# The delta rule's recurrence on one core: products of 64 partitions laid over all 128

## The chip, the cores and the metric

The kernel runs on one core of a Trainium2 chip. The metric is the time on the device in microseconds (us) for one execution, as the median of several runs. Nothing else runs on the chip.

## The reference

The model is two blocks on 512 tokens of 1024 features, in float32: a block with two attention branches and a layer of product-key experts, then a gated delta net and a short convolution. The change lies in the gated delta net alone, in its recurrence. It has 16 value heads that share 8 key heads in pairs, head width 128, and goes over the tokens in 8 chunks of 64:

```python
    def step(s, xs):
        q_c, k_c, u_c, w_c, qk_c, sd_c = xs
        v_new = u_c - jnp.einsum('bhck,bhkv->bhcv', w_c, s)
        o_c = jnp.einsum('bhck,bhkv->bhcv', q_c, s) + jnp.einsum('bhij,bhjv->bhiv', qk_c, v_new)
        s = s * sd_c[..., None, None] + jnp.einsum('bhck,bhcv->bhkv', k_c, v_new)
        return s, o_c
...
    _, o = lax.scan(step, s0, xs)
```

The state `s` of a head is 128 x 128 and is handed from chunk to chunk, so the chunks of a head are serial. `u_c` and `w_c` are the solutions of a 64 x 64 triangular system for each chunk and head.

## The kernel before, in words

One program runs four stages one after the other: `mix`, `peer`, `gdn`, `sconv`. All work of this study is in `gdn`, after its projections of keys and queries and after the inverse of the triangular systems. Tokens lie on partitions in tiles of 128, so one tile holds two chunks: chunk n has the partitions `o`, the lower 64 if n is even (`a_` = 0) and the upper 64 if it is odd (`a_` = 1). `RQ0` and `RQ1` hold for 8 heads each the inverse R (`RQ[:, 0]`) and the masked query-key product Q (`RQ[:, 1]`), as [128 partitions, 32 pairs of head and token tile, 64 columns]: the two chunks of a tile share a column block and lie on the two halves of the partitions.

`recur(kh, ...)` is a generator that takes the two value heads of key head kh through 8 chunks. It yields after each step that waits for another engine, 23 times in all; such a step is called a hop here. For every chunk but the first and last there are three:

- the state's product (L1510): keys and queries of the chunk, [128, 128] as the weights, times the state `Sx` of both heads in one product of 256 columns; then the output of the chunk before (L1495, Q times `vn`). VectorE answers with `rr` (L1513).
- L1518: R times `rr`, from the 64 partitions `o` onto the 64 partitions `o`. ScalarE answers with `vn` (L1519), then with two products for the output (L1522).
- L1529: `kd` times `vn`, from the 64 partitions `o` onto 128. VectorE answers with the new state `sn` (L1536, or L1533 for the first chunk).

The first chunk has no state: its L1518 reads `vb`. All products of the recurrence are float32, and TensorE runs each as two records of a load of weights and a matmul, so that the two heads of a hop make four.

TensorE's instructions stand in the order in which the code emits them (`manual_schedule`). A written plan places the hops: two key heads run at a time, one 12 steps of the plan behind the other, each has one hop in a step, and `fill` puts products of other projections in between: those of values and of the output gate (L207 to L209 on `x3h`, `x3l`: three float32r products of 512 columns for each row tile, 128 x 128 weights), and later of the output (the same lines on `ygh`, `ygl`, 256 columns). `prologue` starts a key head (transposes L1471 and L1480; `va`, the values, come by a DMA that GpSimd issues, L1477; VectorE makes `kd` and `vb`). `epilogue` and `epilogue2` end one (transposes L1558, then `ygh` on ScalarE, L1566). The other engines' order is set by the scheduler of the tile framework. Weights of the projections are loaded by SyncE and split in two parts by ScalarE (`whi`, L89) and VectorE or GpSimd (`wlo`, L92).

Of the kernel before, what the change touches and what calls it, by code (L numbers as in the profile page):

```python
# [29 lines left out]
def kernel(ctx: ExitStack, tc: tile.TileContext, A: dict, out: bass.AP):  # L30
# [24 lines left out]
    # ---------------------------------------------------------------- helpers  # L55
# [21 lines left out]
    share = {"every": 0, "n": 0}    # of the weights' second parts, every n-th by the pool engine  # L77

    def wchunk(ap, name="w"):
        """A [128, 2048] chunk of a weight matrix (8 row tiles, 256 columns) in two halves, each split  # L80
        into two float32r parts. For a token-major product the halves are along the rows, for a
        feature-major one along the columns."""
# [15 lines left out]
    def rsqrt(ss, n, shape, name="rs", dst=None):  # L98
        """1/sqrt(ss*n + eps): a first guess from the exponent's bits, then Newton steps."""
# [16 lines left out]
    def rsqrt2(ss, n, name, dst=None):  # L116
        """the same for two columns on the pool engine, by its power"""
        m = small.tile([P, 2], F32, name=name, tag=name)
        GP.tensor_scalar(m, ss, n, EPS, op0=ALU.mult, op1=ALU.add)
        r = m if dst is None else dst  # L120
        GP.tensor_tensor(r, m, mhalf, op=ALU.pow)
        return r
# [6 lines left out]
    def evac_split(hi, lo, p, scale):  # L129
        """hi + lo = p * scale, in two float32r parts."""  # L130
        S.activation(hi, p, AF.Copy, scale=scale)
        V.scalar_tensor_tensor(lo, p, scale, f32(hi), op0=ALU.mult, op1=ALU.subtract)
# [3 lines left out]
    class Stream:  # L136
        """The residual stream between two stages, [128, 4, 1024] token-major: in SBUF, in DRAM, 1/rms
        of every token, and the normed stream transposed, in two parts [128, 8, 512]. n: the stage
        that reads it."""
# [12 lines left out]
        def squares(self, tiles):  # L152
            """the sums of squares of every token of two token tiles"""
# [6 lines left out]
        def ready(self, t, ss):  # L160
            """token tiles t and t + 1 are complete; ss: their sums of squares"""
# [6 lines left out]
        def norm(self, t):  # L168
            """token tile t, normed and transposed"""
# [20 lines left out]
        def first_feat(self, ap, order=(0, 1)):  # L190
            """The token tiles of the second half, and proj_feat of the first chunk by halves."""
            w = [(m, *kview(x, NK)) for m, *x in wchunk(ap)]
            pp = [pj() for m in range(2)]
            for j in order:
# [4 lines left out]
                # The first start clears the whole bank.  # L199
# [28 lines left out]
    def proj_tok_last(aps, xs):  # L228
        """proj_tok whose token tiles end one after the other; yields them by pairs."""
# [22 lines left out]
    def proj_feat_steps(ap, xh, xl, by, n=T):  # L252
        """feature-major: [128 features, n tokens] for the two column tiles of a chunk."""
# [9 lines left out]
    def proj_tok_steps(aps, xs, by):  # L263
        """token-major: four [128 tokens, 256 columns]; aps: the chunks along K, xs: their operands."""
# [4 lines left out]
        # Two groups share a bank: the first matmul's start clears the whole bank, and the second  # L269
        # group's first write finds it cleared.  # L270
# [12 lines left out]
    # ---------------------------------------------------------------- token mixing  # L283
    def mix(X, O):
        w1 = A["w_in"]
        with ExitStack() as st:
# [56 lines left out]
            # ---- gated linear attention, head by head  # L343
# [5 lines left out]
            def gla_inside(h):  # L349
                """the parts of a head that need no state"""  # L350
# [94 lines left out]
            # ---- sliding window attention  # L445
# [31 lines left out]
            # Keys and queries in two float32r parts, feature-major: the keys' first part twice, on either  # L477
            # half of the partitions, and a query's two parts on the two halves; so one pass gives two of
            # the three products, and a second one the third. The second key head pair has the halves
            # swapped, for its keys' second part lies on the other half.  # L480
# [63 lines left out]
            def weights(n, hg, qT):  # L544
                """the softmax of four heads that share keys; the columns hold the tokens of block n up to the
                row and those of block n - 1 after it"""
# [57 lines left out]
            # ---- branch gates, output gate of the linear attention  # L604
# [31 lines left out]
            # Four heads a slot: their scores in one slot, the weighted sums two slots later; the tensor  # L636
            # engine's work in a fixed order, with the gates' projections in between.
# [31 lines left out]
            # ---- branches, merge  # L669
# [39 lines left out]
    # ---------------------------------------------------------------- product-key experts  # L709
    def peer(X, O):  # L710
        KD = 3                      # token tiles that go through all experts on the tensor engine
        ND = KD * P
        HS = 16                     # tokens of a staged block of gate matrices
        TB = 4                      # tokens of a block of one-hot rows
        with ExitStack() as st:
# [19 lines left out]
            # ---- the last token tile: its experts' rows by indirect DMA  # L735
# [37 lines left out]
            # ---- the other tiles through all experts: groups of five chunks, ten rows of experts  # L773
# [57 lines left out]
            # ---- scores and the 16 best keys of every head and half  # L831
# [36 lines left out]
            def route(t):  # L868
                """the 16 best experts of every head, their gates; yields every few operations"""
# [3 lines left out]
                # pairs (a, b) with (a+1)(b+1) <= 16: every other pair has 16 better or earlier ones  # L873
# [35 lines left out]
                # gates  # L909
# [21 lines left out]
                # indices and the gate's two parts, one row per (head, k), as float16  # L931
# [7 lines left out]
            def gate_matrices(t):  # L939
                """G[j, i] of every token of the tile, expert i * 128 + j"""  # L940
# [26 lines left out]
            # the tensor engine's projections at an even rate in between  # L967
# [41 lines left out]
    # ---------------------------------------------------------------- gated delta rule  # L1009
    def out_proj(aps, parts, X, O, wr, Y=None):  # L1010
        """X + rmsnorm(the projection (+ Y)) * w; aps[c]: the weights of 256 columns."""
# [38 lines left out]
    def conv_silu(p, wc, taps, tmp):  # L1050
        """Causal depthwise convolution along the free axis, one weight per partition and tap."""
# [7 lines left out]
    def gdn(X, O):  # L1059
# [6 lines left out]
        with ExitStack() as st:  # L1066
# [23 lines left out]
            # ---- keys and queries, feature-major and not normed: [dk, head, chunk, (k | q), 64]  # L1090
# [6 lines left out]
            def kq_mm(i):  # L1097
                """one tile of 128 columns of the projection; i: pair of key heads, (k, q), key head"""
# [26 lines left out]
            # ---- beta and g, token-major [128, 4, 16]  # L1125
# [53 lines left out]
            def g_rows():  # L1179
                # E[j, (h, t), i] = exp(G_i - G_j) for j <= i, else 0  # L1180
# [37 lines left out]
            def u_store(c, q):  # L1218
                """the diagonal blocks of U of key heads 2c and 2c + 1"""
# [8 lines left out]
            def rows(c):  # L1228
                """the factors of every token of key heads 2c and 2c + 1"""
# [56 lines left out]
            # ---- values (filler of the triangular solve)  # L1286
# [94 lines left out]
            # ---- R = (I + U)^-1: 32 x 32 diagonal blocks by substitution, (half, head, tile) on  # L1381
            # partitions
# [18 lines left out]
            # to rows on partitions by the tensor engine; the first block's transpose too  # L1401
# [12 lines left out]
            # the off-diagonal blocks: -R1 U12 R2; the two halves' blocks on a diagonal  # L1414
# [70 lines left out]
            def recur(kh, vb, kd, oo):  # L1485
# [15 lines left out]
                for n in range(8):  # L1501
# [26 lines left out]
                    for v in range(2):  # L1528
                        PE.matmul(B2[:, 1, v], kd[o, v, t, :], vn[o, v], start=True, stop=True)  # L1529
# [282 lines left out]
```

## Time and profile before

| what | value |
|---|---|
| median of 3 runs | 3065.36 us (3063.47 to 3077.59) |
| span of the profiled execution | 3072.8 us |
| TensorE busy over the span | 2943.9 us (96%) |
| VectorE, ScalarE, GpSimd busy | 1972.4, 1216.1, 662.6 us |
| recurrence, first to last product | 2246.8 to 2549.0 us of the span |
| TensorE, VectorE, ScalarE busy from 2246 to 2549 us | 294.9, 163.9, 123.2 us of 303.0 |
| mean granted TensorE clock there | 0.95 of full speed |

The profile gives for each instruction its engine, its start and its duration, and for each wait the engine that ended it. A matmul's end is modelled, so what a matmul costs is read from the start of one to the start of the next, or from the chain of work that ended last, in which the pieces follow one another without overlap. No time beyond its span is given for the profiled execution. It is 7.4 us longer than the median and lies within the runs shown.

### The profile page before, as it was taken

How to read it: one execution, taken by the hardware profiler on the slowest of the kernel's cores; microseconds unless marked ns; L12 is line 12 of the kernel's file. 1: busy time of each engine (PE TensorE's matmuls, PEld its weight loads, DVE VectorE, ACT ScalarE, POOL GpSimd, SP SyncE). 2: the span in 40 equal slices, each digit the busy share in tenths (PEclk: the TensorE clock that was granted, in tenths of full speed). 3: DMA queues.
4: the chain of work that ended last, by engine and by line, in shares of the span. 5: the costliest groups of instructions: out<-in, count | busy, mean ns of one | idle time of the engine just before them, and what ended most of it. 6: DMA issues, size and time to landing. Idle time of an engine off the chain costs nothing.

```text
span 3072.8 us, 42867 instructions
## 1 busy us (share of the span) xinstructions
PE 2943.9 (96%) x16274; PEld 2499.6 (81%) x16274; DVE 1972.4 (64%) x3798; ACT 1216.1 (40%) x2089; POOL 662.6 (22%) x583
## 2 busy tenths in 40 slices
PE   8999999998889999999899999999999999999998
PEld 6978778888889998777798888787866678888888
DVE  3348664499898776777787777658845554444432
ACT  3534473323345553333333333465343344332322
POOL 1001110002342312223454443134411202000000
PEclk9999999999999999999999999999999899999999
DMA  3213224333466779899999888446322313223222
GB/s 130 76 58 131 85 86 157 106 100 100 143 217 226 244 267 307 315 333 317 323 315 313 308 320 309 160 115 144 128 86 90 107 59 119 98 96 124 96 90 83
DMA packets 206919, 528.61 MB, mean 172 GB/s; under 512 B 38777, under 2 KB 84441, under 8 KB 202362
## 3 DMA queue, kind: packets, MB, share of 16 engines
q1 hardware_dynamic: 144018, 326.17, 32.5%
q0 software_dynamic: 43168, 155.27, 14.2%
q10 hardware_dynamic: 19528, 44.44, 3.9%
q8 instruction: 128, 2.10, 0.3%
q14 instruction: 77, 0.63, 0.1%
HBM read 464.49 MB, written 61.33 MB: 171 GB/s over the span
## 4 chain that ended last, share of the span: by engine, by line
PE 50%; DMA 9%; DVE 6%; issue 4%; ACT 2%; POOL 1%; SPq 0%; POOLq 0%; DVEq 0%; ACTq 0%
PE pp L207 12%; PE pp L208 11%; PE pp L209 11%; DMA wraw<-in_peer_v_dram 4%; DMA gath<-in_peer_v_rows_dram,ge 2%; PE ps L209 2%; PE ps L208 2%; PE ps L207 2%; DVE wlo L92 1%; PE ps L1495 1%; PE ps L1529 1%; DMA gath<-in_peer_u_rows_dram,ge 1%; DMA wraw<-in_peer_u_dram 1%; PE ps L954 1%; POOL gath L751 1%
## 5 line engine op out<-in xcount | busy, mean ns | idle before, releaser
L89 ACT ACTIVATE whi<-wraw 128x1024 fp32r<-128x1024 f32 x492 | 519.9, 1057 | 980.1 <-PE pp L208 555.1
L92 DVE TENSOR_TENSOR wlo<-wraw,whi 128x1024 fp32r<-128x1024 f32 x466 | 580.3, 1245 | 422.6 <-ACT whi L89 409.7
L209 PE MATMUL pp<-x2h,wlo 128*128 128x384 f32 (+2 forms) x1168 | 405.4, 347 | 23.7 <-DVE wlo L92 22.0
L207 PE MATMUL pp<-x2h,whi 128*128 128x384 f32 (+2 forms) x1168 | 407.6, 349 | 17.3 <-ACT whi L89 9.7
L208 PE MATMUL pp<-x2l,whi 128*128 128x384 f32 (+2 forms) x1168 | 404.2, 346 | 1.1 <-DVE x2l L188 1.1
L209 PE MATMUL ps<-whi,wtl 128*128 128x512 f32 x640 | 254.8, 398 | 8.5 <-DVE wtl L817 8.5
L208 PE MATMUL ps<-wlo,wth 128*128 128x512 f32 x640 | 254.9, 398 | 3.2 <-DVE wlo L92 3.2
L207 PE MATMUL ps<-whi,wth 128*128 128x512 f32 x640 | 253.8, 397 | 2.3 <-ACT whi L89 2.0
L209 PEld LDWEIGHTS pp<-x2h,wlo 128*128 128x128 f32 x1168 | 224.8, 193 | 34.7 <-DVE wlo L92 28.1
L751 POOL DMA_INDIRECT gath<-in_peer_u_rows_dram,ge x128 | 173.3, 1354 | 336.2 <-DVE gath L754 168.6
L207 PEld LDWEIGHTS pp<-x2h,whi 128*128 128x128 f32 x1168 | 225.3, 193 | 24.2 <-ACT whi L89 10.8
L751 POOL DMA_INDIRECT gath<-in_peer_v_rows_dram,ge x128 | 170.1, 1329 | 316.9 <-DVE gath L754 153.7
L208 PEld LDWEIGHTS pp<-x2l,whi 128*128 128x128 f32 x1168 | 225.2, 193 | 6.5 <-DVE x2l L188 1.6
L207 PE MATMUL pp<-x4h,whi 128*128 128x512 f32 (+1 forms) x528 | 202.4, 384 | 3.8 <-ACT x4h L187 3.8
L208 PE MATMUL pp<-x4l,whi 128*128 128x512 f32 (+1 forms) x528 | 202.7, 384 | 0.9 <-DVE x4l L188 0.9
L209 PE MATMUL pp<-x4h,wlo 128*128 128x512 f32 (+1 forms) x528 | 202.5, 384 | 0.0
L759 DVE SCALAR_TENSOR_TENSOR acc<-gath,w,acc 128x1024 f32<-128x1024 f32 x127 | 163.7, 1289 | 22.7 <-DMA gath<-in_peer_v_rows_dram,ge 22.5
L754 DVE SCALAR_TENSOR_TENSOR gath<-gath,grow 128x1024 f32<-128x1024 f32 x128 | 157.4, 1237 | 30.0 <-DMA gath<-in_peer_u_rows_dram,ge 29.8
L207 PE MATMUL pp<-x3h,whi 128*128 128x512 f32 (+1 forms) x400 | 168.4, 421 | 7.4 <-ACT x3h L187 5.7
L816 ACT ACTIVATE wth<-wt 128x384 fp32r<-128x384 f32 x128 | 66.8, 522 | 252.1 <-PE pp L208 154.5
L208 PE MATMUL pp<-x3l,whi 128*128 128x512 f32 (+1 forms) x400 | 156.4, 391 | 1.8 <-DVE x3l L188 1.8
L209 PE MATMUL pp<-x3h,wlo 128*128 128x512 f32 (+1 forms) x400 | 156.3, 391 | 0.0
(492 smaller groups left out, 6500.2 us busy)
## 6 DMA issues: line engine op xcount, KB each, us to landing
wraw<-in_peer_u_dram SPq DMA_DIRECT2D x128, 512.0 KB, 5.3
wraw<-in_peer_v_dram SPq DMA_DIRECT2D x128, 512.0 KB, 7.1
wraw<-in_sc_w_in_dram SPq DMA_DIRECT2D x64, 512.0 KB, 3.5
wraw<-in_w_in_dram SPq DMA_DIRECT2D x52, 512.0 KB, 4.0
Gd<-sgs ACTq DMA_DIRECT2D x24, 1024.0 KB, 6.5
wraw<-in_gdn_w_in_dram SPq DMA_DIRECT2D x48, 512.0 KB, 3.7
Gt<-Gd SPq DMA_DIRECT2D x12, 1920.0 KB, 15.8
Hd<-ht ACTq DMA_DIRECT2D x25, 384.0 KB, 4.5
```

Source lines behind the costliest of these rows:

```text
L89: S.activation(hi, raw, AF.Copy)
L92: (GP if pool_ else V).tensor_tensor(lo, raw, f32(hi), op=ALU.subtract)
L207: PE.matmul(p, lh, rh, start=first, stop=False, skip_group_check=skip)
L208: PE.matmul(p, lh, rl, start=False, stop=False, skip_group_check=skip)
L209: PE.matmul(p, ll, rh, start=False, stop=last, skip_group_check=skip)
L751: GP.indirect_dma_start(out=r, out_offset=None, in_=src, in_offset=bass.IndirectOffsetOnAxis(ap=idx3[:, k:k + 1], axis=0))
L754: V.scalar_tensor_tensor(r, r, 1.0, xn3, op0=ALU.mult, op1=ALU.mult, accum_out=h3[:, k:k + 1])
L759: V.scalar_tensor_tensor(acc3, r, w3[:, k:k + 1], acc3, op0=ALU.mult, op1=ALU.add)
L816: S.activation(wh, w, AF.Copy)
L954: PE.matmul(o, AB[:, 1, :, q], A2[:, 0, :, q], start=True, stop=False)
L1495: PE.matmul(B2[o, 0, v], Q[s_][o, u, :], vn[o, v], start=True, stop=True)
L1529: PE.matmul(B2[:, 1, v], kd[o, v, t, :], vn[o, v], start=True, stop=True)
```

## The change

Every product of the recurrence is made a product of 128 partitions onto 128. Two tiles for each of the two lanes (a lane is kh odd or even) and each parity of the chunk take the place of `rr` and `vn`: `rz` and `vz`. Their other half is set to zero once, by GpSimd, before the recurrence; each chunk writes its own half alone. `wide_mm` then takes 128 columns of `RQ` as weights: the chunk's own block of 64 and the block beside it, on the side that puts the wanted result on the chunk's own half of the output. The other half of the output receives a product that nobody reads. The first or last block of `RQ0` and `RQ1` has no such neighbour: there the product stays one of 64 output partitions (L1502). `kd` is taken on all 128 partitions, with the zeros of `vz` against the other chunk. The state's product of 256 columns becomes two of 128, one for each head. The first chunk's right side is now copied from `vb` into `rz` by VectorE (L1527). Comments and empty lines changed in many other places; they are left out here.

```diff
+            lanes = []
+            for i in range(2):
+                lanes.append([[tp.tile([P, 2, P], F32, name=n, tag="%s%d%d" % (n, i, a_)) for a_ in range(2)]
+                              for n in ("rz", "vz")])
+                for x in lanes[i]:
+                    for a_ in range(2):
+                        GP.memset(x[a_][64 * (1 - a_):64 * (1 - a_) + 64], 0.0)
+            RQ = [x.rearrange("p x u c -> p (x u c)") for x in (RQ0, RQ1)]
+
+            def wide_mm(out_, s_, u, a_, rhs):
+                c = 64 * (u - a_)
+                if 0 <= c <= 62 * 64:
+                    PE.matmul(out_, RQ[s_][:, c:c + P], rhs, start=True, stop=True)
+                else:
+                    PE.matmul(out_[64 * a_:64 * a_ + 64], RQ[s_][:, 64 * u:64 * u + 64], rhs, start=True, stop=True)
...
+                rz, vz = lanes[kh % 2]
...
-                        PE.matmul(B2[o, 0, v], Q[s_][o, u, :], vn[o, v], start=True, stop=True)
+                        wide_mm(B2[:, 0, v], s_, 32 + u, n % 2, vn[:, v])
...
-                    vn = r1("vn", 4)
+                    vn, r = vz[a_], rz[a_]
                     if Sx is None:
-                        r = vb[:, :, t, :]
+                        V.tensor_copy(r[o], vb[o, :, t, :])
                     else:
-                        r = r1("rr", 2)
-                        PE.matmul(B1[:, 0].rearrange("p v c -> p (v c)"), k_[:, n].rearrange("p x c -> p (x c)"),
-                                  Sx.rearrange("p v c -> p (v c)"), start=True, stop=True)
+                        for v in range(2):
+                            PE.matmul(B1[:, 0, v], k_[:, n].rearrange("p x c -> p (x c)"), Sx[:, v], start=True,
+                                      stop=True)
...
-                        PE.matmul(B1[o, 1, v], R[s_][o, u, :], r[o, v], start=True, stop=True)
+                        wide_mm(B1[:, 1, v], s_, u, a_, r[:, v])
...
-                        PE.matmul(B2[:, 1, v], kd[o, v, t, :], vn[o, v], start=True, stop=True)
+                        PE.matmul(B2[:, 1, v], kd[:, v, t, :], vn[:, v], start=True, stop=True)
```

On TensorE, at the start of the recurrence, the first hops of key head 0 stand so before the change (out<-in, output partitions x columns; `vn` and `rr` are the right sides, `RQ`, `kd` and `kq` the weights):

```order
L209 MATMUL pp<-x3h,wlo 128x512
L1518 MATMUL ps<-vb,RQ_17371 64x128 x2
L207 MATMUL pp<-x3h,whi 128x512
L208 MATMUL pp<-x3l,whi 128x512
L209 MATMUL pp<-x3h,wlo 128x512
L1529 MATMUL ps<-vn,kd 128x128 x2
...
L1510 MATMUL ps<-sn,kq_17370 128x256
L1495 MATMUL ps<-vn,RQ_17371 64x128 x2
```

and so after it:

```order
L209 MATMUL pp<-x3h,wlo 128x512
L1500 MATMUL ps<-rz,RQ_17371 128x128 x2
L207 MATMUL pp<-x3h,whi 128x512
L208 MATMUL pp<-x3l,whi 128x512
L209 MATMUL pp<-x3h,wlo 128x512
L1549 MATMUL ps<-vz,kd 128x128 x2
...
L1530 MATMUL ps<-sn,kq_17370 128x128 x2
L1500 MATMUL ps<-vz,RQ_17371 128x128 x2
```

Nothing moved on TensorE: each hop keeps its place between the same products of the projections, and only the shapes are others.

On GpSimd, between the inverse and the recurrence, the zeros stand ahead of the first loads of values:

```order
 L1419 MEMSET Tc 64x64x32 x2
 L92 TENSOR_TENSOR wlo<-wraw,whi 128x1024
-L1477 DMA va<-vd 128x512 x2
-L1560 DMA zl<-zd 128x512 x3
+L1494 MEMSET rz 64x256 x2
+L1494 MEMSET vz 64x256 x2
+L1494 MEMSET rz 64x256 x2
+L1494 MEMSET vz 64x256 x2
+L1477 DMA va<-vd 128x512 x2
+L1580 DMA zl<-zd 128x512 x3
```

The two loads `va`, which the first L1480 waits for, now stand behind eight more instructions.

On TensorE, where the two lanes meet without a projection between them and one chunk is the last block of its tile set, the rows after the change are these (`RQ_17371` is `RQ0`, `RQ_17392` is `RQ1`):

```order
L209 MATMUL pp<-x3h,wlo 128x512
L1530 MATMUL ps<-sn,kq_17370 128x128 x2
L1500 MATMUL ps<-vz,RQ_17371 128x128
L1502 MATMUL ps<-vz,RQ_17371 64x128
L1530 MATMUL ps<-sn,kq_17391 128x128 x2
```

One of four such products that keep their 64 output partitions stands here (L1502).

## Rows read from the trace of the kernel before

**Rows 1.** The page's head: busy us by engine (share of the span), instructions.

```profile
span 3072.8 us, 42867 instructions
PE 2943.9 (96%) x16274; PEld 2499.6 (81%) x16274; DVE 1972.4 (64%) x3798; ACT 1216.1 (40%) x2089; POOL 662.6 (22%) x583
```

**Rows 2.** Windows: length, busy (xcount) of PE, PEld, DVE, ACT, POOL; granted clock; DMA.

```profile
2246.00:2549.00 303.00, 294.91 (x1668) 207.49 (x1666) 163.93 (x445) 123.16 (x360) 43.41 (x53) 0.95 0.26 84
2344.00:2354.30 10.30, 9.78 (x30) 6.27 (x31) 2.98 (x8) 2.30 (x7) 1.14 (x3) 0.50 0.51 170
2419.00:2439.60 20.60, 20.59 (x63) 13.68 (x63) 5.57 (x18) 2.55 (x9) 2.67 (x5) 0.50 0.33 103
```

**Rows 3.** The chain that ended last: start us, us, what (records).

```profile
2302.89 1.02 PE ps L1480 x8
2303.92 0.23 PE pp L207
...
2304.62 0.64 PE ps L1529 x4
2305.26 0.43 PE pp L207
...
2306.15 0.57 PE ps L1510 x2
2306.72 0.58 PE ps L1495 x4
2307.29 0.43 PE pp L207
...
2308.19 0.87 PE ps L1558 x8
2309.06 0.58 PE ps L1518 x4
2309.64 0.43 PE pp L207
```

**Rows 4.** Waits, 2245 to 2550 us: who <- releaser: us, times, longest.

```profile
PEld pp L207 <- issue: 17.7, 96, 0.3
PEld ps L1529 <- ACT vn L1519: 7.2, 9, 1.6
PE ps L1529 <- ACT vn L1519: 4.1, 5, 1.4
```

**Rows 5.** The same chain where hops of both lanes meet.

```profile
2367.24 0.43 PE ps L1510 x2
2367.68 0.25 PE ps L1495
2367.93 0.01 PE ps L1518
2367.94 0.09 PE ps L1495
```

**Rows 6.** The chain at the start of key head 3.

```profile
2339.99 0.12 PE ps L1558
...
2344.09 0.39 ACT vn L1519
...
2344.52 1.22 PE ps L1529 x4
```

**Rows 7.** Ahead of the recurrence: timeline, a group by line, the tile va.

```profile
2237.88 1.16 POOL L1477 DMA_DIRECT2D va<-vd  x2
...
2242.79 1.30 PE L1480 MATMUL ps<-ident,va 128*128 128x128 f32 x8
...
L1421 POOL MEMSET Z<- 64x256 f32 x8 | 2.3, 308 | 0.1
...
DMA to landing us min/median/max: 4.0/4.4/4.8
```

**Rows 8.** Groups by line, VectorE, 2246 to 2549 us.

```profile
L1533 DVE COPY sn<-ps 128x128 f32<-128x128 f32 x16 | 4.0, 284 | 3.3 <-PE ps L1529 3.3
```

## The prediction

> **What bounds the kernel now.** I read the page's head first: TensorE is busy 96% of the span, no other engine over 64% [rows 1]. Then the windows of the recurrence: of 303.0 us TensorE is busy 294.9, VectorE 163.9, ScalarE 123.2 [rows 2]. So the stage ends when TensorE has issued its list, and the recurrence's serial answers are mostly covered by the projections between the hops. Busy is no proof of useful work, though, so I read the chain that ended last, whose pieces don't overlap [rows 3]. There the reader should compare two kinds of neighbours of the same projection. After a hop whose products use 64 rows or 64 columns of the array, L207 takes 0.43 us; after transposes that use all 128 x 128 (L1480 x8) it takes 0.23, which is its streaming. And four records of L1518 take 0.58, four of L1495 0.58, four of L1529 0.64, where eight float32 records of 128 columns with 128 x 128 weights (L1558 x8) take 0.87, 0.109 each. The dear thing is not the small product but going into and out of its shape. The waits agree: TensorE's weight loads stand idle before L207 96 times, 17.7 us in all, for "issue", which is nothing that the profile shows; of the waits that name another engine the longest are 7.2 us of weight loads and 4.1 of matmuls, both L1529 for ScalarE's `vn` [rows 4].
>
> **The change part by part.** *Shape switches removed.* One visit to a small hop costs 0.58 + 0.43 = 1.01 us with the L207 behind it [rows 3]. In full shape it is four records of 0.109, 0.44, and L207 at 0.23: 0.67. That saves 0.34. For L1529 it is 0.64 + 0.43 - 0.67 = 0.40. For the state's hop, L1510 x2 takes 0.43 where it needn't wait [rows 5], so 0.43 + 0.58 + 0.43 = 1.44 becomes eight records, 0.87, and 0.23: again 0.34. The two products of 128 columns cost what one of 256 did, 0.44 for 0.43. In TensorE's order of the program I count 156 runs of small hops between full-shape rows (184 hops, some next to each other), 42 of them entered by L1529. That gives 156 x 0.34 + 42 x 0.06 = 55.6 us. Seven of the runs end in the transposes L1471, whose 64 output columns stay another shape; their way out, 0.20, isn't saved: -1.4. Gross 54.2.
>
> *Side by side lost.* In six places an L1495 of one lane and an L1518 of the other follow each other on opposite halves. There the records alternate at 0.01 and 0.09 [rows 5]: eight take 0.56, and in full shape they take 0.87 one after the other. With L207 that is 0.99 now and 1.10 then: a loss of 0.11 where I booked a gain of 0.34, so I take off 6 x 0.45 = 2.7 us. [...] At its most, with all 512 records of R and Q two at a time, the loss would be 512 / 2 x 0.109 = 28 us instead of 2.7. But the four records of one visit don't overlap in the chain (0.58 for four), since both heads use the same half, so the sum goes by the row. [...]
>
> *Four products that keep 64 columns* (L1502): in and out of the shape again, 4 x 0.34 = 1.4 us lost.
>
> *Zeros ahead of the values.* Eight fills of 64 x 256 go in front of the first two loads `va` in GpSimd's queue. A fill of this shape takes 0.308 us [rows 7], together 2.5. `va` lands 4.0 to 4.8 us after its issue at 2237.9, so by 2242.7 at the latest, and L1480 starts at 2242.8: up to 0.9 us of slack. TensorE's order is fixed, so it stands still for 1.6 to 2.5 us; I take 2.0. GpSimd idled long before, but the fills stand behind its share of the weights in the queue. Nothing behind `va` is urgent (`zl` is for the epilogue).
>
> *Eight copies into `rz`.* 64 x 256 has no row; the nearest is a copy of 128 x 128 out of PSUM, 0.284 us [rows 8]. A first L1500 now waits for it, but it has three steps of the plan between `vb` and that product; the bounds are 0 and 8 x 0.28 = 2.3. I take 1.0, since VectorE may have other work before it.
>
> *Where the stall goes.* TensorE takes 303 us for about 116 steps of the plan, 2.6 us a step, and comes to a lane's next hop one step later. An answer is one or two operations of some 0.3 us plus what the engine has before them. With two visits cheaper in each step the next hop is due 0.4 to 0.7 us earlier, which a slack near 1 us mostly covers. Where it doesn't, the saving is lost: at the start of key head 3 the chain leaves TensorE at 2340.1, runs through VectorE and ScalarE (`ygh`, `whi`, `vn`) and comes back at 2344.5 [rows 6]. Those 4.4 us don't shrink, and the switches saved beside them, about three, become waiting; the order on ScalarE there is the same after the change. TensorE stands idle 303.0 - 294.9 = 8.1 us in the stage [rows 2]. Bounds of what is added: nothing, and 24 us (0.15 us for each of some 160 hops). I take 6, nearer to the first, for VectorE would be busy 163.9 of some 260, 63%, and ScalarE 47%.
>
> **The sum.** 54.2 - 2.7 - 1.4 - 2.0 - 1.0 - 6.0 = 41.1 us. The profiled execution would go from a span of 3072.8 to 3031.7. It is 7.4 above the median of the runs; from 3065.4 I get 3024. [...]
>
> **The rivals.** *The answers bind* (0.14): the recurrence was balanced against TensorE's list as it was, and a faster list meets late `rr`, `vn`, `sn` at most hops. Then 24 instead of 6 us is lost: 3042. For it: L1529 already waits 4.1 and 7.2 us [rows 4]; against it: VectorE is idle 46% of the stage.
>
> *The clock* (0.22 in all): without the two slow stretches, 3024 - 14.8 = 3009 (0.13), since nothing small is left; with one more like the longer, from the wait for `va` or a longer one for `vn`, 3024 + 9.9 = 3034 (0.09).
>
> *The switch has another cause* (0.03): if the 0.20 came from going between float32 and float32r, it would stay, and only the costs 2.0 + 1.0 + 2.7 remain: 3071. Against it stands L1480 x8, float32, with L207 at 0.23 behind it [rows 3].
>
> *Records of full shape cost more* (0.03), the other side: the 0.109 is read from transposes. If a float32 product with its own 128 x 128 weights had to load them (another 0.109) before it streams, each of the 960 records of the recurrence (8 key heads x 30 products of two heads x 2 x 2) would take 0.218 and the change would cost 960 x 0.109 = 105 us against 41: 3129. It decides from 0.043 more a record on. Against it: L1510 streams 256 columns with two loads in 0.43, no more than 4 x 0.109.
>
> *Side by side at its most* (0.01): the 28 us above in place of 2.7, 3049.
>
> **How the numbers follow.** My forecast has 0.57, by its own bounds 3014 to 3034. The range 3006 to 3043 takes in the clock's cases and the binding answers, and leaves out the last three rivals and tails. Faster by over 0.5% (below 3050, about what runs that spread from 3063 to 3078 can tell) is all but the last three and a little of the tails: 0.92; within 0.5% 0.04; slower 0.04.
>
> **What would show it.** In the changed profile: L207 behind a hop at 0.23 in the chain; L1500 and L1549 at 0.109 a record; some 260 us from the first to the last product of the recurrence; L1480 of key head 0 about 2 us late; idle time of TensorE in the stage near 16 us, most of it for `vn` and `sn`. Wrong would make me a full-shape record well over 0.109, waits over 30 us, or slow stretches much longer than 31 us.

## The result, and the profile after

Median 3019.48 us after (4 runs, 3008.92 to 3028.42) against 3071.48 before (4 runs, 3063.47 to 3083.01): ratio 0.9837, 95% interval 0.9808 to 0.9865, 52.0 us between the medians. Forecast were 3024 us and 41.1 us. Run again beside the first experiments, the change gave a ratio of 0.9817, interval 0.978 to 0.9855. Two single runs far off the rest, 12090 us of the kernel before and 4472 us of e7 at granted clocks of 0.22 and 0.58, are left out of every ratio. The profiled execution took 3028.42 us, its span is 3026.3. First the page's head, which answers to [rows 1]:

```profile
span 3026.3 us, 43065 instructions
PE 2896.7 (96%) x16386; PEld 2514.2 (83%) x16386; DVE 1974.3 (65%) x3806; ACT 1215.4 (40%) x2089; POOL 667.1 (22%) x591
```

TensorE works 47 us less, and the span is 46.5 us shorter. The windows of the recurrence come next, from the start of its first product to the start of its last, and the one stretch in it at the low clock; the columns are those of [rows 2]:

```profile
2252.70:2501.40 248.70, 238.03 (x1775) 215.16 (x1774) 165.81 (x452) 122.42 (x360) 42.27 (x53) 0.99 0.31 101
2339.40:2342.80 3.40, 3.40 (x14) 3.01 (x13) 1.36 (x5) 0.00 (x0) 0.91 (x2) 0.50 0.77 234
```

The stage takes 248.7 us; by the same marks it took 302.0 before (2246.8 to 2548.8, inside the window of [rows 2]). That is 53.3 us less, more than the whole difference of the spans: what comes ahead of the stage took 6.0 us longer in this execution (1.5 of them are the wait for `va` below), and what comes behind it 0.9. In the traces of this study the stage starts anywhere from 2235 to 2253 us, before and after the change alike, and the rest behind it takes 524 to 527. So kernels are compared below by this stage, and by the ratios of their runs. At 0.50 the stage spent 3.4 us, and 30.7 before. Where a length "at full clock" is given, half of the time at 0.50 is taken off, which is an estimate (from the start of L208 to that of L209 it is 0.43 us in the stretches at 0.50 before, 0.23 outside them): 302.0 - 15.3 = 286.7 before and 248.7 - 1.7 = 247.0 after, 39.8 us apart. The other 53.3 - 39.8 = 13.5 us are the clock.

The chain that ended last, the place that answers to [rows 3]:

```profile
2308.00 0.45 PE ps L1500 x4
2308.45 0.23 PE pp L207
...
2310.28 1.08 PE ps L1549 x8
2311.36 0.23 PE pp L207
...
2312.06 0.44 PE ps L1530 x4
2312.50 0.45 PE ps L1500 x4
...
2313.84 0.23 PE pp L207
```

L207 behind a hop takes 0.23 us and no longer 0.43. Four records of a hop take 0.44 to 0.45, 0.112 each, where the transposes of [rows 3] gave 0.109. The state's hop, L1530 and L1500, is 0.44 + 0.45 + 0.23. The waits of TensorE's matmuls, 2200 to 2550 us, as in [rows 4]:

```profile
PE ps L1549 <- ACT vz L1539: 5.7, 6, 1.8
PE ps L1530 <- DVE sn L1556: 2.3, 4, 1.2
PE ps L1480 <- DMA va<-vd: 1.5, 2, 1.1
PE ps L1500 <- DVE rz L1533: 1.1, 1, 1.1
```

The 96 waits of weight loads before L207 for "issue", 17.7 us, are gone from the top of this view. What is left is waiting for answers: `vz` (5.7 us now, `vn` 4.1 before), `sn`, `rz`. Over the stage, TensorE's idle time rose from 7.9 to 10.5 us. Last the timeline (start, duration, engine, instruction, and the idle time before it), which answers to [rows 7] and shows one visit start by start:

```profile
2242.65 0.67 POOL L1494 MEMSET rz<- 64x256 f32 x2
...
2244.79 0.67 POOL L1494 MEMSET vz<- 64x256 f32 x2
2245.41 1.16 POOL L1477 DMA_DIRECT2D va<-vd  x2
...
2248.53 0.63 PE L1480 MATMUL ps<-ident,va 128*128 128x128 f32 x4 [1.13 <-DMA va<-vd]
2249.53 0.63 PE L1480 MATMUL ps<-ident,va 128*128 128x128 f32 x4 [0.37 <-DMA va<-vd]
...
2308.75 0.39 PE L209 MATMUL pp<-x3h,wlo 128*128 128x512 f32 x1
2308.99 0.60 PE L1500 MATMUL ps<-rz,RQ 128*128 128x128 f32 x4
2309.35 0.48 PE L207 MATMUL pp<-x3h,whi 128*128 128x512 f32 x1
2309.66 0.40 PE L208 MATMUL pp<-x3l,whi 128*128 128x512 f32 x1
```

The eight fills take 2.8 us ahead of `va` in GpSimd's queue, and L1480 starts 1.13 + 0.37 = 1.5 us late; 2.0 was forecast. The visit of four L1500 costs 2309.66 - 2308.75 = 0.91 us from the start of L209 to that of L208.

A visit is what stands between two products of the projections: one hop, or several in a row. TensorE's order is the same in both kernels, so its 145 visits can be matched one by one. Where neither trace has a wait or a low clock in the visit, the median visit of R or Q alone is 0.324 us shorter (34 visits), of the update 0.384 (31), of the state with Q 0.315 (27).

### The profile page after: what moved, and what is told of

It reads as the page before. It is cut to its first block, busy times and chain, and to the rows that moved or that the text cites. A ratio compares the mean times of both kernels' runs of the same rounds, so it can differ in the third digit from the quotient of the medians.

```text
span 3026.3 us, 43065 instructions
## 1 busy us (share of the span) xinstructions
PE 2896.7 (96%) x16386; PEld 2514.2 (83%) x16386; DVE 1974.3 (65%) x3806; ACT 1215.4 (40%) x2089; POOL 667.1 (22%) x591
## 3 DMA queue, kind: packets, MB, share of 16 engines
q0 software_dynamic: 43168, 155.27, 14.5%
## 4 chain that ended last, share of the span: by engine, by line
PE 49%; DMA 8%; DVE 6%; issue 5%; ACT 2%; POOL 2%; POOLq 0%; DVEq 0%; ACTq 0%
PE pp L207 11%; PE pp L208 11%; PE pp L209 11%; DMA wraw<-in_peer_v_dram 3%; PE ps L209 3%; PE ps L208 2%; PE ps L207 2%; DMA gath<-in_peer_v_rows_dram,ge 2%; PE ps L1500 2%; DMA gath<-in_peer_u_rows_dram,ge 1%; POOL gath L751 1%; DVE wlo L92 1%; DMA wraw<-in_peer_u_dram 1%; PE ps L954 1%; PE ps L955 1%
## 5 line engine op out<-in xcount | busy, mean ns | idle before, releaser
L209 PE MATMUL pp<-x2h,wlo 128*128 128x384 f32 (+2 forms) x1168 | 406.2, 348 | 23.1 <-DVE wlo L92 19.6
L207 PE MATMUL pp<-x2h,whi 128*128 128x384 f32 (+2 forms) x1168 | 409.3, 351 | 17.3 <-ACT whi L89 8.6
L208 PE MATMUL pp<-x2l,whi 128*128 128x384 f32 (+2 forms) x1168 | 405.9, 348 | 0.7 <-DVE x2l L188 0.7
L209 PE MATMUL ps<-whi,wtl 128*128 128x512 f32 x640 | 255.7, 400 | 7.7 <-DVE wtl L817 7.5
L208 PE MATMUL ps<-wlo,wth 128*128 128x512 f32 x640 | 255.4, 399 | 2.3 <-DVE wlo L92 2.2
L207 PE MATMUL ps<-whi,wth 128*128 128x512 f32 x640 | 254.6, 398 | 2.2 <-ACT whi L89 2.2
L209 PEld LDWEIGHTS pp<-x2h,wlo 128*128 128x128 f32 x1168 | 226.2, 194 | 34.0 <-DVE wlo L92 25.9
L207 PEld LDWEIGHTS pp<-x2h,whi 128*128 128x128 f32 x1168 | 226.7, 194 | 24.1 <-ACT whi L89 9.6
L208 PEld LDWEIGHTS pp<-x2l,whi 128*128 128x128 f32 x1168 | 226.6, 194 | 6.1 <-DVE x2l L188 1.3
L207 PE MATMUL pp<-x4h,whi 128*128 128x512 f32 (+1 forms) x528 | 202.9, 385 | 3.8 <-ACT x4h L187 3.8
L208 PE MATMUL pp<-x4l,whi 128*128 128x512 f32 (+1 forms) x528 | 203.2, 385 | 0.6 <-DVE x4l L188 0.4
L209 PE MATMUL pp<-x4h,wlo 128*128 128x512 f32 (+1 forms) x528 | 202.8, 384 | 0.0
L207 PE MATMUL pp<-x3h,whi 128*128 128x512 f32 (+1 forms) x400 | 164.5, 411 | 7.4 <-ACT x3h L187 5.7
L208 PE MATMUL pp<-x3l,whi 128*128 128x512 f32 (+1 forms) x400 | 154.6, 387 | 1.6 <-DVE x3l L188 1.6
L209 PEld LDWEIGHTS ps<-whi,wtl 128*128 128x128 f32 x640 | 121.5, 190 | 40.4 <-DVE wtl L817 12.5
```

The lines of the kernel that those rows point to most:

```text
L207: PE.matmul(p, lh, rh, start=first, stop=False, skip_group_check=skip)
L208: PE.matmul(p, lh, rl, start=False, stop=False, skip_group_check=skip)
L209: PE.matmul(p, ll, rh, start=False, stop=last, skip_group_check=skip)
```

## The experiments

Twelve kernels on three chips, each beside its own runs of the kernel before on the same chip. Stage: first to last product of the recurrence in the trace, as above.

| run | ratio, 95% interval | stage, us | at 0.50 | at full clock | TensorE idle |
|---|---|---|---|---|---|
| before (trace) | | 302.0 | 30.7 | 286.7 | 7.9 |
| a1_before | 0.9995 [0.9975, 1.0014] | 300.6 | 27.3 | 287.0 | 7.9 |
| a0_change | 0.9817 [0.978, 0.9855] | 248.6 | 3.4 | 246.9 | 10.5 |
| e1_state_one | 0.9829 [0.9793, 0.9865] | 253.3 | 3.4 | 251.6 | 14.9 |
| e2_kd_half | 0.9857 [0.982, 0.9894] | 259.4 | 0 | 259.4 | 8.0 |
| e3_half_out | 0.9907 [0.9874, 0.9941] | 275.3 | 0 | 275.3 | 11.1 |
| e4_half_in | 0.9946 [0.9927, 0.9965] | 279.8 | 0 | 279.8 | 8.3 |
| e5_late_vz | 0.9908 [0.9886, 0.9929] | 270.3 | 10.2 | 265.2 | 24.7 |
| e6_no_half_late_zero | 0.9839 [0.9816, 0.9862] | 246.0 | 0 | 246.0 | 10.8 |
| e7_64x64 | 0.9939 [0.9919, 0.996] | 284.6 | 20.5 | 274.4 | 10.7 |
| e8_before_late_vn | 1.0082 [1.0053, 1.0111] | 340.1 | 99.0 | 290.6 | 14.5 |
| e9_before_split | 0.9992 [0.9974, 1.0009] | 297.1 | 23.9 | 285.1 | 7.0 |
| e10_vz_first | 0.9796 [0.9768, 0.9824] | 240.9 | 0 | 240.9 | 6.9 |

**The two kernels again.** a0_change is the changed kernel as it is, a1_before the kernel before.

> The changed kernel again, for its time beside the runs below and for a second trace of its clock. Theory (a change of the array's shape costs about 0.34 us for in and out, 156 times): ratio to before 0.983 to 0.988, recurrence near 249 us from its first to its last product. Rival (13 of the 53 us that the recurrence lost were the slow clock stretches of one execution, so the change itself is worth 40): the ratio's middle is 0.987, and the stretches at 0.50 differ from the first trace's 3.4 us.

> The kernel before once more, for a second trace of its recurrence. Theory (the stretches at 0.50 of its recurrence come from small products and waits together): again 10 to 35 us at 0.50 between its first and last product. Rival (chance of one execution): any amount, also none, and then the recurrence takes near 288 us instead of 302.

Both repeat; the change's ratio is a little under the 0.983 to 0.988 that was expected, and its interval reaches into it. In a1_before the two slow stretches stand at the same two places as in [rows 2], the starts of key heads 3 and 5, 10.6 us earlier, as the stage starts 10.9 earlier. They are, in its windows:

```profile
2333.40:2343.60 10.20, 9.92 (x30) 6.41 (x31) 2.73 (x8) 2.08 (x6) 1.10 (x2) 0.50 0.48 163
2408.50:2425.60 17.10, 17.10 (x51) 11.30 (x51) 4.31 (x14) 2.15 (x7) 2.67 (x5) 0.50 0.39 124
```

In a0_change one stretch of 3.4 us is left, at the start of key head 3, as in the trace above. The wait at which the first stretch begins is there in both kernels (before, then after):

```profile
2344.52 1.22 PE L1529 MATMUL ps<-vn,kd 64*128 64x128 f32 x4 [1.44 <-ACT vn L1519]
2338.51 0.71 PE L1549 MATMUL ps<-vz,kd 128*128 128x128 f32 x4 [1.80 <-ACT vz L1539]
```

It is longer after the change, and the slow stretch at it is shorter, 3.4 us instead of 10.3. All runs together agree: the mean granted clock of the whole span is 0.985 to 0.988 in the nine runs of the change, and 0.974 to 0.988, 0.983 in the mean, in 60 runs of the kernel before. So the loss of slow time is no accident of one execution.

**Which part of the shape costs.** Three edits give a part of the old shape back: the update's rows (e2), R's and Q's output columns (e3), R's and Q's rows (e4).

```diff
# e2_kd_half
-                        PE.matmul(B2[:, 1, v], kd[:, v, t, :], vn[:, v], start=True, stop=True)
+                        PE.matmul(B2[:, 1, v], kd[o, v, t, :], vn[o, v], start=True, stop=True)
# e3_half_out: all products of R and Q by the branch that four took
-                if 0 <= c <= 62 * 64:
+                if False:
# e4_half_in (in the other branch likewise)
-                    PE.matmul(out_, RQ[s_][:, c:c + P], rhs, start=True, stop=True)
+                    PE.matmul(out_, RQ[s_][64 * a_:64 * a_ + 64, c:c + P], rhs[64 * a_:64 * a_ + 64], start=True, stop=True)
```

> The changed kernel with the third product of a chunk (kd times the new values) on 64 partitions again, still onto 128; R and Q stay full. Theory: 50 separate runs of it, each 0.40 us for going into the 64-row shape and out: recurrence near 269 us, L207 behind it at 0.43 instead of 0.23 in the chain. Rival (the gain came from the R and Q products or from the clock): at most 5 us longer.

> The changed kernel with R's and Q's products contracted over 128 partitions but onto 64 output partitions; the rest full. Theory (any change of shape costs, also of columns alone): 114 separate runs of 0.34 us, recurrence near 288 us. Rival (only the rows count, a product of 64 columns is free to sit among full ones): 249 us within 3.

> The changed kernel with R's and Q's products over 64 partitions but onto 128 output partitions (weights of 128 columns); the rest full. Theory (any change of shape costs, also of rows alone): 114 separate runs of 0.34 to 0.40 us, recurrence 288 to 294 us. Rival (only the columns count): 249 us within 3.

At full clock they are 12.4, 28.3 and 32.8 us longer than the change (a0_change and the trace after: 247.0); 20, 39 and 39 to 45 were expected. The same visit as in the timeline above, L209, four records of R, L207, L208, in e3:

```profile
2316.54 0.40 PE L209 MATMUL pp<-x3h,wlo 128*128 128x512 f32 x1
2316.86 0.65 PE L1502 MATMUL ps<-rz,RQ 128*64 128x128 f32 x4
2317.45 0.50 PE L207 MATMUL pp<-x3h,whi 128*128 128x512 f32 x1
2317.78 0.39 PE L208 MATMUL pp<-x3l,whi 128*128 128x512 f32 x1
```

and in e4, where the rows ahead of the "..." show a visit in which both lanes meet:

```profile
2295.78 0.37 PE L1500 MATMUL ps<-vz,RQ 64*128 64x128 f32 x1
2295.80 0.37 PE L1500 MATMUL ps<-rz,RQ 64*128 64x128 f32 x1
...
2312.51 0.40 PE L209 MATMUL pp<-x3h,wlo 128*128 128x512 f32 x1
2312.83 0.71 PE L1500 MATMUL ps<-rz,RQ 64*128 64x128 f32 x4
2313.47 0.50 PE L207 MATMUL pp<-x3h,whi 128*128 128x512 f32 x1
2313.81 0.39 PE L208 MATMUL pp<-x3l,whi 128*128 128x512 f32 x1
```

From L209's start to L208's: 0.91 us in full shape, 2317.78 - 2316.54 = 1.24 with half the columns, 1.30 with half the rows. By matched visits against the change the medians are +0.327 (e3, 34 visits), +0.384 (e4, 35), +0.384 (e2, 32 updates). One half small is as dear as both (0.324, e7 below). So neither rows alone nor columns alone are the cause; every change of shape tried here has its price. In the visits shown the first record of R starts 0.32 us after L209 in e3 and e4, 0.24 in full shape, and L207 0.59 and 0.66 us after that record, 0.36 in full shape. That the sums are less than the number of runs by these prices has two grounds in the traces: in e2 TensorE waited 2.5 us less, as the answers had more time, and where both lanes' products meet they run side by side again, in e3 (0.01 us apart at 2293.76) as in e4 (the rows at 2295.78: 0.02 us apart). Whether these two cover all that is missing isn't shown.

**All of R and Q small again, the rest as after the change.**

```diff
# e7_64x64, in place of wide_mm's two branches
+                b = slice(64 * a_, 64 * a_ + 64)
+                PE.matmul(out_[b], RQ[s_][b, 64 * u:64 * u + 64], rhs[b], start=True, stop=True)
```

> The change with R's and Q's products 64 rows by 64 columns again, as before it (each from its own half of the partitions onto its own half); the update of the state stays over 128 partitions and the state's product stays split. What is open is why the stretches at clock 0.50 within the recurrence shrank from 27 to 31 us to 3.4 us, when the runs with rows alone, columns alone or the update alone had none. Theory: the 64 by 64 products themselves go with the low clock. Then the stage shows 15 to 31 us at 0.50 at the starts of key heads, and at full clock is 276 to 282 us long (as with columns alone or rows alone), with the low clock 284 to 296; ratio to before 0.994 to 1.000. Rival: the low clock needs all the old shapes together, or the waits at the starts of key heads as they fell before: then at most 4 us at 0.50, 276 to 282 us long, ratio 0.990 to 0.995. [...]

The timeline of such a visit, and the windows of its stage and of its longer slow stretch:

```profile
2309.52 0.40 PE L209 MATMUL pp<-x3h,wlo 128*128 128x512 f32 x1
2309.85 0.65 PE L1499 MATMUL ps<-rz,RQ 64*64 64x128 f32 x4
2310.42 0.51 PE L207 MATMUL pp<-x3h,whi 128*128 128x512 f32 x1
2310.77 0.40 PE L208 MATMUL pp<-x3l,whi 128*128 128x512 f32 x1
```

```profile
2241.60:2526.20 284.60, 273.75 (x1775) 215.83 (x1775) 167.66 (x452) 122.84 (x360) 42.84 (x53) 0.96 0.27 88
2373.70:2390.80 17.10, 16.56 (x55) 13.01 (x56) 4.68 (x15) 4.25 (x13) 2.22 (x4) 0.50 0.22 77
```

The visit costs 2310.77 - 2309.52 = 1.25 us, by matched visits 0.324 more than in the change (34 visits), like e3's. The theory's test was the clock, and it holds: 20.5 us at 0.50, where e3 has none:

```profile
2248.80:2524.20 275.40, 264.18 (x1776) 209.41 (x1775) 167.66 (x452) 122.76 (x360) 42.79 (x53) 1.00 0.29 91
```

At full clock the two are 0.9 us apart, 274.4 and 275.3 (a little under the 276 that was expected). The stages differ by 284.6 - 275.3 = 9.3 us, all of it clock. The times of the runs don't show it: the ratios differ by 0.0032, 10 us of 3070, but the two ran on different chips and their intervals overlap, and the whole spans of the two traces are only 2.0 us apart, as e3's execution has 81.5 us at 0.50 outside the stage and e7's 64.6. The mean granted clock of the runs agrees with the stages: 0.986 to 0.989 in e3's six, 0.982 to 0.986 in e7's eight.

**How late the answers may be.** e5 adds to the change, e8 to the kernel before, one more ScalarE copy ahead of each copy of the solved values.

```diff
+                    vj = small.tile([P, D], BF16, name="njunk", tag="njunk", bufs=1)[o, :256]
+                    S.activation(vj.rearrange("p (v c) -> p v c", v=2), B1[o, 1], AF.Copy)
                     S.activation(vn[o], B1[o, 1], AF.Copy)
```

> The changed kernel with one more ScalarE operation of 64 x 256 (0.38 us) in front of each of the 64 answers vz, writing what nobody reads. Theory (an answer has slack near 1 us in most steps, so the recurrence is still bound by TensorE's list): at most 8 of the 24 us show. Rival (after the change the answers bind): 20 us or more.

> The kernel before, with one more ScalarE copy of the same 64 x 256 numbers into a scratch tile ahead of each copy of vn, some 0.4 us later for each of 64 answers. The same addition to the change made its recurrence 18 us longer at full clock (24 us of copies). Theory: in the kernel before the answers had more time, since every hop of TensorE between them took some 0.34 us longer; the added copies cost at most 10 us there (ratio at most 1.0035), and TensorE's idle time in the stage rises from 8 to at most 16 us. Rival: the slack was as small before as after; 15 to 22 us (1.005 to 1.007), idle 22 us or more.

In both the stage holds 58 more ScalarE operations and 16.5 us more ScalarE work. After the change all of it comes through and a little more: 265.2 - 247.0 = 18.2 us at full clock. The theory of e5, at most 8, failed; its rival, 20 or more, was nearly reached. Its waits on `vz`, and its windows (the stage, and the 10 us ahead of the second of its three slow stretches):

```profile
PEld ps L1551 <- ACT vz L1541: 15.0, 20, 1.8
PE ps L1551 <- ACT vz L1541: 9.6, 14, 1.6
```

```profile
2241.10:2511.40 270.30, 245.47 (x1778) 217.90 (x1776) 166.88 (x452) 138.91 (x418) 43.09 (x53) 0.98 0.30 93
2360.30:2370.30 10.00, 6.33 (x38) 4.75 (x37) 8.99 (x18) 4.81 (x10) 4.75 (x4) 1.00 0.40 139
```

In the kernel before the same work costs 290.6 - 286.7 = 3.9 us at full clock, so the longer hops had hidden it: the theory holds for the slack. It fails for the time. The stage's windows, the 10 us ahead of the longest slow stretch, and that stretch:

```profile
2240.20:2580.30 340.10, 325.41 (x1665) 225.14 (x1664) 163.78 (x445) 139.51 (x418) 43.20 (x53) 0.85 0.23 74
2388.30:2398.30 10.00, 7.74 (x43) 5.00 (x42) 7.36 (x20) 4.70 (x10) 4.66 (x4) 1.00 0.33 107
2398.30:2435.80 37.50, 36.64 (x117) 23.80 (x118) 9.78 (x30) 11.59 (x40) 4.82 (x9) 0.50 0.32 98
```

The low clock went from 30.7 to 99.0 us, 34 us of stage, in the slowest of this kernel's six runs (3083.81 to 3108.94); over the runs it is 1.0082, 25 us. e5 had more waiting ahead of its slow stretch (TensorE busy 6.33 of 10 us against 7.74 here) and more idle time in all (24.7 against 14.5), and its three slow stretches ended after 3.4 us each. What differs between the two kernels is the shape of the products and the split of the state's; e9, which has the split and the old shapes, holds 23.9 us at 0.50.

**The state's product, split or whole.** e1 takes the split back from the change, e9 makes it alone in the kernel before.

```diff
# e1_state_one; e9_before_split is the reverse
-                        for v in range(2):
-                            PE.matmul(B1[:, 0, v], k_[:, n].rearrange("p x c -> p (x c)"), Sx[:, v], start=True,
-                                      stop=True)
+                        PE.matmul(B1[:, 0].rearrange("p v c -> p (v c)"), k_[:, n].rearrange("p x c -> p (x c)"),
+                                  Sx.rearrange("p v c -> p (v c)"), start=True, stop=True)
```

> The changed kernel with the state's product as one of 256 columns again, all else full shape. Theory: nothing in TensorE's list changes in length (0.43 against 4 x 0.11), so the recurrence stays at 249 us within 2. Rival (two products of 128 columns let VectorE begin on the first head 0.2 us earlier, and that is part of the gain): 3 to 6 us longer, and more idle time of TensorE behind VectorE's right sides.

> The kernel before, with the state's product alone in two products of 128 columns. After the change the split was worth 4.7 us, by shorter waits (VectorE begins on the first head while the second is still computed). Theory: the same here, 3 to 6 us less (ratio 0.998 to 0.999), idle time of TensorE in the stage from 8 to 4 us or less. Rival: the old shapes leave VectorE the time that the split gains, since the next hop is later anyway; within 2 us, idle unchanged.

The waits of e1's matmuls:

```profile
PE ps L1529 <- DVE sn L1555: 6.2, 11, 1.5
PE ps L1548 <- ACT vz L1538: 5.7, 6, 1.8
```

TensorE's busy time in the stage is the same with the product whole or split (238.26 and 238.03 us). But `sn` is waited for 11 times, 6.2 us, where the change shows 4 times and 2.3, while the one wait for VectorE's right side `rz` is 1.1 us in both. So the gain isn't the one that both expectations name, VectorE beginning earlier on the first head. It is TensorE that begins earlier: VectorE writes the new state one head after the other, and with two products the first can start when the first head's state is there. In the change's trace:

```profile
2256.11 0.38 PE L1530 MATMUL ps<-sn,kq 128*128 128x128 f32 x2
2256.80 0.49 PE L1530 MATMUL ps<-sn,kq 128*128 128x128 f32 x2 [0.31 <-DVE sn L1553]
```

VectorE's copy of the second head ends at 2256.75, between the two. In 28 of the 56 visits of the state the first product starts so, before VectorE has ended the second head; a single product (before, e1) reads both heads and can't. That is worth 251.6 - 247.0 = 4.6 us after the change. In the kernel before it happens in 8 of the 56 (e9), is worth 1.6 to 1.9 us at full clock, and the ratio has 1 in its interval. The expectation that it matters nowhere fell in e1, the one that it matters everywhere fell in e9.

**Two mends.** e6 makes the zeros of a lane after that lane's first loads are queued, and spares the four products of 64 columns by giving two chunks the other half; e10 also puts ScalarE's copy of `vz` ahead of its other work.

```diff
# e6_no_half_late_zero
                             vb, kd = prologue(kh)
+                            if kh < 2:
+                                lane(kh)
...
# e10_vz_first, besides
+                    with tc.high_priority(offset=1000):
+                        S.activation(vn[o], B1[64 * side:64 * side + 64, 1], AF.Copy)
```

> The changed kernel with two of its own costs taken out: the four products that kept 64 output partitions take the block on the other side and their result from the other half, and each lane's zeros are written behind the first loads of values in GpSimd's queue instead of ahead of them. Theory: 4 x 0.34 = 1.4 us and the wait of the first L1480 for va (1.5 us) go, about 3 us in the trace, too little for the median to tell. Rival (the zeros or their tiles cost more than that wait, for instance at the first right side): over 8 us.

> The change with zeros by lane as they are needed and no half products (measured: 1.0 us less in the stage), and ScalarE's copy of vz ahead of ScalarE's other ready work. Theory: half of TensorE's idle time in the recurrence (10.8 us) waits for vz behind other ScalarE work; it falls to 5 to 7 us, and the time by 4 to 6 us against the change (ratio to before 0.980 to 0.982). Rival: the waits for vz are the copy's own latency, or the waits move to what ScalarE then does later; within 2 us, ratio 0.982 to 0.985.

e6 saves 1.0 us of the stage at full clock, and ahead of the stage the wait for `va` falls from 1.5 to 0.3 us; about 3 us were expected, and the runs can't show so little. e10 saves 5.1 more in the stage. Its stage, and two of its matmuls' waits:

```profile
2243.60:2484.60 241.00, 233.95 (x1776) 213.65 (x1775) 164.48 (x452) 122.40 (x360) 44.94 (x58) 1.00 0.34 108
```

```profile
PE ps L1530 <- DVE sn L1558: 3.2, 5, 1.5
PE ps L1551 <- ACT vz L1541: 0.3, 1, 0.3
```

Waits of L1551 for `vz` have gone from 5.6 us in e6 to 0.3, and idle time from 10.8 to 6.9. With 0.9796, interval 0.9768 to 0.9824, it has the lowest ratio here: its stage is 7.7 us shorter than the change's in the trace, 6.1 at full clock. Its runs were on another chip than the change's, whose intervals overlap with it, so the gain over the change rests on the stage.

## Why the prediction was right, and where it was off

The forecast of 3024 us is 4.5 us from the median, inside its own bounds of 3014 to 3034. The nearness is in part luck. The median before rose by 6.1 us with its fourth run, and the gain, 41.1 forecast, lies at the edge of what the ratio's interval allows (41.5 to 59.0 us). Errors of opposite sign helped too. The sum against what the trace shows: 41.1 forecast; 7.7 less from switches, 4.4 more from waits, 0.5 more from `va`, 13.5 more from the clock; 51.8, which is the stage's 53.3 less the 1.5 for `va`.

- **Shape switches removed**: right in kind, a little large in size. Forecast 0.34 us for a run of R, Q or the state with Q, and 0.40 for the update; the matched visits show 0.324, 0.315 and 0.384. The full record is 0.112 us and not 0.109, which is 960 x 0.003 = 2.9 us. Net of lanes side by side and the four L1502, 50.1 us of TensorE's time was forecast and 39.8 + 2.6 = 42.4 came. Of the 7.7 missing, about 3 are this price (156 runs by 0.02). The rest sits among the 26 visits that hold a wait or the low clock in one of the traces; there the matching can't divide them, and taking half of the time at 0.50 is itself an estimate.
- **In and out of the shape**: every change of shape has a price in the runs, for rows alone (0.384 us a visit), columns alone (0.327) and both (0.324); what TensorE does in that time they don't show.
- **Zeros ahead of the values**: 2.0 forecast, 1.5 measured. **Copies into `rz`**: 1.0 forecast; no wait for them (L1527) shows in the change's trace, and the 1.1 us for `rz` above are for L1533, the right side of a later chunk.
- **Where the stall goes**: 16 us of idle time forecast, 10.5 measured. The forecast booked the split of the state's product at nothing, as it does cost nothing on TensorE; without it (e1) the idle time is 14.9, 7.0 more than before, which is what was booked (6.0 + 1.0). The reason was only half right: "which a slack near 1 us mostly covers" holds for the change itself, but it used that slack up. The chain at the start of key head 3 did stay 4.4 us long (2334.1 to 2338.5), and TensorE's wait at its end grew from 1.44 to 1.80 us. The same delay of an answer costs 3.9 us before the change and 18.2 after.
- **The step that failed**: the sum has no term for the clock, so the forecast carries the two stretches of [rows 2] at 0.50, 10.3 and 20.6 us, over as they were. They shrank to one of 3.4 us. The wait at which the first begins doesn't carry it: the wait is still there, 1.80 us instead of 1.44, and the low clock ends after 3.4 us. In every trace here with products of 64 x 64 in R and Q the stage holds 20 to 99 us at 0.50 (before, a1_before, e7, e8, e9); in every trace without them (e4 has four) 0 to 3.4, and 10.2 in e5, which waits most. e7 and e3 differ in this alone (R's and Q's rows), and the clock differs. The rival "without the two slow stretches" had the reason, "nothing small is left", at 0.13. No run shows the 14.8 and 9.9 us with which the two cases of the clock are reckoned; the traces showed 30.7 us at 0.50 before and 3.4 after, by half of the time 13.5 us of stage.
- **The other rivals**: the answers bind at few hops in the change as it is (10.5 us idle), and a few tenths of a us more make them bind at many (e5). The switch has no other cause: with all types as they were, e3 and e4 have 0.327 and 0.384 us of it back in each visit. Full records cost what transposes do but for 0.003 us. Side by side was worth what was forecast: in the four visits where opposite halves meet without a wait or a low clock in either trace, the change is 0.10 to 0.12 us longer, and 0.11 was booked. e3 and e4 have it back, and are slower.

## What to carry to other kernels

Where TensorE is busy all the time, compare a visit of small products between two large ones with one of full-shape products, from start to start; the difference, here 0.32 to 0.38 us for each visit, was paid with half the columns (e3, 0.327) as with half the rows (e4, 0.384), so full shape paid here only with both sides filled. When TensorE's list gets shorter, look again at what the answering engines do first: putting one answer first on ScalarE was worth 5 us after the change (it was not tried before it), and a delay that the kernel before mostly hid (3.9 us of 16.5 came through) came through whole after it (18.2). And a stretch at a low clock is not a constant to be carried over (30.7 us of the stage before, 3.4 after): ask which products stand in it.

## What the runs showed of the hardware that was not expected

- With R and Q in 64 x 64, stretches at 0.50 lasted up to 37.5 us (e8); with 128 x 64, 64 x 128 or 128 x 128 in their place none in the stage was over 3.4 us (e3, e4; the change, e5). By waits alone e5 (24.7 us idle, 10.2 at 0.50) would have come out worse than e8 (14.5 idle, 99.0 at 0.50). Nor does TensorE's busy time ahead of a stretch sort the two: it was 6.33 of the 10 us ahead of one of 3.4 us in e5, and 7.74 of the 10 us ahead of the one of 37.5 in e8. Why the smallest shape goes with the low clock isn't settled here.
- A small delay cost more than itself: 16.5 us more of ScalarE work in the kernel before cost 3.9 us at full clock and 34 by the clock in the profiled execution, the slowest of six; over the runs it is 25 us in all.
- Half shapes of the two lanes run side by side too: in e4 two products of 64 rows each onto all 128 columns start 0.01 to 0.02 us apart, as the 64 x 64 ones of [rows 5] do.
